# First layer's feed-forward: block products for the latents, and a second pass for the context tokens

## The chip, the cores and the metric

The kernel runs on one core of one Trainium2 chip. The metric is device microseconds of one execution. A core has five instruction streams that run beside each other and wait for each other by semaphores: PE (TensorE, matmuls), DVE (VectorE), ACT (ScalarE), POOL (GpSimd) and SP (SyncE, which here only issues DMAs). A weight load of TensorE shows as PEld.

## The reference

Two layers over 1024 noisy latent tokens and 256 context tokens of width 1024 in float32. What matters here is the feed-forward that ends each layer, and the norm at the start of the next:

```python
def modulate(x, shift, scale):
    return rms_norm(x) * (1.0 + scale) + shift

def squared_relu_mlp(h, w1, w2):                 # w1 1024 x 4096, w2 4096 x 1024
    return jnp.square(jax.nn.relu(h @ w1)) @ w2
...
    x = x + gate * squared_relu_mlp(modulate(x, shift, scale), w1, w2)
```

Shift, scale and gate come from a conditioning vector for the latents and from a second, learned one for the context (columns 0 and 1 of `mods`). The first layer's mixer is attention beside an mLSTM, the second's an RWKV-7 scan. The context is needed through the first layer's feed-forward, since the second layer's mixer reads it; after that only the latents go on.

## The kernel before

Activations lie transposed: eight tiles `xt[c]` of 128 channels by 1280 tokens (`NT`; `NL` = 1024 latents, then `NX` = 256 context tokens; `KC` = 8). Each float32 product is made of three: operands are split into a high part in fp32r (ScalarE, L94) and the remainder (GpSimd or VectorE, L95), and hi x hi, lo x hi and hi x lo are summed in PSUM. `load_w` fetches 512 KB of weights into a `raw` buffer, splits it into `wh` and `wl`, and sets `raw` free when GpSimd's subtraction is through.

Each engine runs its instructions in the order in which the program issues them; the tile pools add the waits and hand out buffers. So the order of calls in the code is the order on each engine.

- The first layer's output projection (`out0`, products `wo`) adds to x; `Stats.add` sums squares of four groups of tokens (ScalarE squares, TensorE `st` matmuls with ones), `Stats.rstd` makes a root (ScalarE), a reciprocal (VectorE), four broadcast matmuls `rb` and copies.
- The first layer's feed-forward (`mlp_layer`, `mlp`) normalizes all 1280 tokens into `h`, and walks 32 blocks of 128 hidden channels. For each block: 8 x 3 products of w1 over chunks of 512, 512 and 256 tokens (`first`, PSUM `m1`), relu and square on ScalarE, the remainder on VectorE, then 8 x 3 x 3 products of w2 (`second`, `m2`) and an update of x on VectorE (L280) for each. That makes 2 x 32 x 8 x 3 x 3 = 4608 matmuls, all at L110. The modulation weights of the next layer are woven in by a generator, `side` (`ada_w`: 32 pieces of 512 KB, products `ada`, transposes `adat`). `done` stores x to DRAM (`xd`) and sums its squares.
- `layer1_mixer` then loads constants, takes the rstd, and normalizes x in 24 pieces (`norm_h`) between the first projections of the RWKV mixer (products `po`).
- The second layer's feed-forward, on the 1024 latents alone, is `wino_mlp`: the matrices are cut into 2 x 2 blocks, and seven block products with sums and differences of blocks stand for eight (the scheme of Strassen and Winograd). `h_blocks` normalizes x and makes the seven left operands `b0..b6` (a high and a low part of four tiles each), on VectorE, ScalarE and GpSimd. `left_first` makes the right operands from w1 on GpSimd; `wino_first` (products `wa` to `we`) and `wino_second` (products `w`, blocks of w2) do 1344 matmuls of 512 columns each. The hidden blocks go through DRAM (`hd`); `wino_second` runs 64 steps, four groups `s` of 16, and adds the group's results to x at a group's end (`add`, L1260).

Of the kernel before, what the change touches and what calls it, by code (L numbers as in the profile page):

```python
# [6 lines left out]
F32 = mybir.dt.float32  # L7
# [21 lines left out]
def drain(g):  # L29
    for _ in g:  # L30
        pass
# [145 lines left out]


class Stats:

# [14 lines left out]

    def rstd(self):
# [5 lines left out]
        out = kk.slab(self.n, F32, "rstd")  # L202
        for g in range(4):
            pb = kk.bank("rb")
            kk.nc.tensor.matmul(pb[:, :q], kk.row0[32 * g:32 * g + 32, :], r4[32 * g:32 * g + 32, :], start=True, stop=True, tile_position=(32 * g, 0))
            kk.nc.scalar.activation(out[:, q * g:q * g + q], pb[:, :q], AF.Copy)
        return out
# [143 lines left out]
NB = 14  # L351
NSA = 6
# [601 lines left out]

def out0(kk, I, xt, cat, mods):
# [12 lines left out]
    return st  # L968
# [46 lines left out]
def h_blocks(kk, xt, mods, part, rstd, B):  # L1015
# [15 lines left out]
    def norm(c, i, p=None):  # L1031
        x = half(c, i)
        s1, b1 = mods[:, 8 * part + 8 + c, 0:1], mods[:, 8 * part + c, 0:1]
        V.tensor_tensor(x, x, rstd[:, 512 * i:512 * i + 512], ALU.mult)
        if p is not None:
            nc.scalar.activation(B[p][c % 4][0], x, AF.Identity, scale=s1, bias=b1)
        V.tensor_scalar(x, x, s1, b1, ALU.mult, ALU.add)
        if p is not None:
            low(p, c % 4, x)
# [136 lines left out]
def wino_second(kk, w2, hd, late, pool, xr, gate, done):  # L1176
# [64 lines left out]
    ready = [operands(0), operands(1)]  # L1241
    for c in range(KC):
        nc.sync.dma_start(xt[c], xr[c])
    g1 = lambda c: gate[:, c, 0:1]
    for i, (s, f) in enumerate(steps):
        load(i + LO2)
        if i + 2 < len(steps):
            ready.append(operands(i + 2))
# [9 lines left out]
        def add(c, h, t):  # L1258
            x = xt[c][:, 512 * h:512 * h + 512]
            V.scalar_tensor_tensor(x, t, g1(c), x, ALU.mult, ALU.add)  # L1260
            return x
        for c in range(4):
            if s == 0:
                A.activation(u[c], banks[0][c], AF.Copy)
            elif s in (1, 2):
                V.tensor_tensor(u[c], banks[0][c], u[c], ALU.add)  # L1266
        for c in range(4):
            if s == 0:
                V.tensor_tensor(v[c], banks[1][c], u[c], ALU.add)
                done(add(c, 0, v[c]), c, 0)  # L1270
            elif s == 1:
                A.activation(v[c], banks[1][c], AF.Copy)
                add(c, 1, v[c])
                add(c, 1, u[c])
            elif s == 2:
                t = kk.tmp([128, 512], "r12", bufs=2)
                V.tensor_tensor(t, u[c], banks[1][c], ALU.subtract)  # L1277
                done(add(4 + c, 0, t), 4 + c, 0)
                add(4 + c, 1, u[c])
                done(add(4 + c, 1, v[c]), 4 + c, 1)  # L1280
            else:
                done(add(c, 1, banks[0][c]), c, 1)
        banks = None


def wino_mlp(kk, X, xt, mods, w1, w2, stats, xr, done):

# [32 lines left out]

def norm_h(kk, xt, mods, h, rstd):

    nc = kk.nc
    for c in range(KC):
        for z in (0, 257, 1282):
            nc.gpsimd.memset(h[c][:, z:z + 1], 0.0)
        for a, b, cond, to in ((NL, NT, 1, 1), (0, 512, 0, 258), (512, NL, 0, 770)):
            t, o = stage(kk, b - a), h[c][:, to:to + b - a]
            nc.vector.tensor_tensor(t, xt[c][:, a:b], rstd[:, a:b], ALU.mult)
            s1, b1 = mods[:, 8 + c, cond:cond + 1], mods[:, c, cond:cond + 1]  # L1330
            if c in NP:
                nc.vector.tensor_scalar(o, t, s1, b1, ALU.mult, ALU.add)
            else:
                nc.scalar.activation(o, t, AF.Identity, scale=s1, bias=b1)
        xt[c] = None
        yield


# [783 lines left out]
def build_full(tc, I, out):  # L2122
    nc = tc.nc
    with tc.tile_pool(name="cst", bufs=1) as cst, tc.tile_pool(name="ps", bufs=8, space=PS) as ps, tc.tile_pool(name="dr", bufs=1, space=DRAM) as dr:
        kk = setup(tc, I, cst, ps, dr)
        cat = layer0_all(kk, I)
        xd = dr.tile([8, 128, NT], F32, name="xd")
        X = tc.alloc_tile_pool(name="X", reuse_waits="tile", bufs=KC)
        with tc.tile_pool(name="W2", reuse_waits="tile", bufs=4) as kk.W:
            xt = load_x(kk, I["xT"], X)  # L2130
            st = out0(kk, I, xt, cat, kk.mods[0])
            kk.WO.release()
            kk.CT.release()
            kk.c0.release()
            st1 = Stats(kk, NT, "mr", 4)

            def done(c):
                nc.sync.dma_start(xd[c], xt[c])
                for x in xt[c - 2:c - 1 if c < KC - 1 else KC] if c >= 2 else []:
                    st1.add(x)  # L2140
# [33 lines left out]

def layer1_mixer(kk, I, xt, X, mods, stats=None):

    tc, nc = kk.tc, kk.nc
    CP = tc.alloc_tile_pool(name="C1", reuse_waits="tile", bufs=1, side="right")
    kk.cst1 = CP
    rwkv_consts(kk, I)  # L2180
    dr, C = rwkv_dram(kk), kk.c
    Hp = tc.alloc_tile_pool(name="H1", reuse_waits="tile", bufs=1, side="right")
    h = [Hp.tile([128, 1283], F32, name="h%d" % c) for c in range(KC)]
    kk.L = X
    kk.wsz = 512
    with tc.tile_pool(name="W1", reuse_waits="tile", bufs=WB) as W, tc.tile_pool(name="XS", reuse_waits="tile", bufs=2 * XA) as S, tc.tile_pool(name="T1", reuse_waits="tile", bufs=2) as T:
        kk.W, kk.S, kk.T, kk.slab_w = W, S, T, NT
        norm = norm_h(kk, xt, mods, h, (stats or rms_of(kk, xt)).rstd())
        C["cmask"] = T.tile([128, 512], mybir.dt.bfloat16, name="cmask", tag="cmask", bufs=1)
# [228 lines left out]
```

## Time and profile before

| | us |
|---|---|
| median of three runs (lowest, highest) | 4336.38 (4334.75, 4348.33) |
| the profiled execution | 4338.47 |
| its span (first to last instruction on the core) | 4336.7 |
| TensorE busy in it | 3998.0 |
| VectorE, ScalarE, GpSimd busy | 2544.1, 1754.5, 1653.5 |
| mean granted TensorE clock | 0.946 of full speed |

A row of a timeline gives start, duration, engine, line, operation, output <- inputs, shapes and count of a merged run of like instructions, and in brackets the idle time ahead and what ended it. A row of groups gives busy us, mean ns of one, and the idle time ahead of them by what ended it. A row of waits names the tile that was waited for and the instruction that gave it: us in total, times, longest.

### The profile page before, as it was taken

What the parts mean: (1) busy time and instruction counts of PE and PEld (TensorE: products, weight loads), DVE (VectorE), ACT (ScalarE), POOL (GpSimd) and SP (SyncE); (2) the same over time, 40 slices, a digit from 0 to 9 for tenths busy, and PEclk for the clock granted to TensorE, in tenths of its full rate; (3) what the DMA queues carried; (4) which work ended last, traced back from release to release, by engine and by line L of the source; (5) the groups of instructions that cost most, each with busy time, mean ns of one, the idle gap of its engine ahead of it and who ended that gap; (6) DMA issues with size and microseconds to landing.
All of it is one profiled execution on the core that took longest, in us unless ns stands there. A gap on an engine that the chain in (4) does not pass through costs nothing. (4 is left out here: it accounts for less than half of the span.)

```text
span 4336.7 us, 71515 instructions
## 1 busy us (share of the span) xinstructions
PE 3998.0 (92%) x26893; PEld 3196.1 (74%) x26893; DVE 2544.1 (59%) x4559; ACT 1754.5 (40%) x4371; POOL 1653.5 (38%) x1827
## 2 busy tenths in 40 slices
PE   6999998998999999997989995999999996998999
PEld 3899875676777888884757764888777764787777
DVE  4320266517556666668684427677777635767673
ACT  4132365513111111125655533666656642332443
POOL 4112010114111111115533335455545325886776
PEclk9999998999999999998979996999989998999999
DMA  4414245511222111112233454445444441345653
GB/s 172 122 61 139 88 156 146 183 35 39 83 83 65 38 36 38 39 39 70 99 117 111 150 191 117 114 126 133 131 123 130 105 160 63 132 159 212 196 168 109
DMA packets 434406, 485.71 MB, mean 112 GB/s; under 512 B 154908, under 2 KB 310844, under 8 KB 434060
## 3 DMA queue, kind: packets, MB, share of 16 engines
q1 hardware_dynamic: 432908, 476.95, 35.4%
q8 instruction: 212, 3.47, 0.3%
q0 software_dynamic: 1152, 4.19, 0.2%
q14 instruction: 134, 1.10, 0.1%
HBM read 347.71 MB, written 129.12 MB: 110 GB/s over the span
## 5 line engine op out<-in xcount | busy, mean ns | idle before, releaser
L95 POOL TENSOR_TENSOR wl<-raw,wh 128x1024 fp32r<-128x1024 f32 (+1 forms) x172 | 354.9, 2067 | 1350.6 <-ACT wh L94 1307.5
L280 DVE SCALAR_TENSOR_TENSOR x<-m,mods,x 128x512 f32<-128x512 f32 (+1 forms) x768 | 467.5, 655 | 341.0 <-PE m L110 340.7
L94 ACT ACTIVATE wh<-raw 128x1024 fp32r<-128x1024 f32 (+1 forms) x172 | 153.8, 895 | 840.0 <-PE m L110 645.6
L110 PE MATMUL m<-h,wh 128*128 128x512 f32 (+1 forms) x1536 | 352.5, 362 | 12.4 <-POOL h L229 9.7
L110 PEld LDWEIGHTS m<-h,wh 128*128 128x128 f32 x1536 | 256.3, 189 | 88.9 <-issue 26.8
L1012 PE MATMUL w<-t,rh 128*128 128x512 f32 x896 | 289.8, 402 | 23.1 <-DVE t L95 12.2
L377 PE MATMUL pt<-wh,h 128*128 128x256 f32 x1600 | 289.3, 283 | 0.0
L95 POOL TENSOR_TENSOR rl<-raw,rh 128x512 fp32r<-128x512 f32 x160 | 232.8, 1459 | 89.7 <-ACT rh L94 85.3
L377 PEld LDWEIGHTS pt<-wh,h 128*128 128x128 f32 x1600 | 250.0, 192 | 0.0
L1821 DVE TENSOR_TENSOR prd<-P,R 80x31 f32<-80x31 f32 (+15 forms) x496 | 217.4, 438 | 25.7 <-POOL TT L1836 7.9
L377 PE MATMUL pt<-wl,h 128*128 128x256 f32 x800 | 226.4, 283 | 0.0
L1012 PEld LDWEIGHTS w<-t,rh 128*128 128x128 f32 x896 | 171.8, 192 | 70.5 <-DVE t L95 17.5
L1822 DVE TENSOR_TENSOR R<-R,prd 80x31 f32<-80x31 f32 (+15 forms) x496 | 216.2, 436 | 9.6
L94 ACT ACTIVATE rh<-raw 128x512 fp32r<-128x512 f32 x160 | 100.7, 632 | 281.7 <-PE w L1012 114.8
L1343 POOL TENSOR_TENSOR ss<-h 128x512 f32<-128x512 f32 (+1 forms) x128 | 153.8, 1211 | 122.0 <-DVE xt L1346 97.1
L110 PE MATMUL m<-hidh,wh 128*128 128x512 f32 (+1 forms) x768 | 198.3, 360 | 1.9 <-DVE x L280 1.9
L110 PE MATMUL m<-hidl,wh 128*128 128x512 f32 (+1 forms) x768 | 195.6, 358 | 0.4 <-DVE hidl L267 0.4
L1782 PE MATMUL G<-AR,BK 64*128 64x128 f32 x1280 | 175.6, 339 | 21.0 <-POOL AR L1771 10.2
L110 PE MATMUL m<-hidh,wl 128*128 128x512 f32 (+1 forms) x768 | 193.7, 357 | 0.0
L110 PE MATMUL m<-h,wl 128*128 128x512 f32 (+1 forms) x768 | 192.9, 358 | 0.0
L1789 DVE TENSOR_TENSOR G<-G,c_gmask 128x512 f32<-128x512 f32 (+1 forms) x160 | 98.8, 630 | 149.9 <-PE G L1782 149.8
L1012 PE MATMUL w<-t,rl 128*128 128x512 f32 x448 | 178.7, 399 | 0.2 <-POOL rl L95 0.2
(708 smaller groups left out, 10446.7 us busy)
## 6 DMA issues: line engine op xcount, KB each, us to landing
raw<-in_w SPq DMA_DIRECT2D x98, 512.0 KB
araw<-in_ada_w SPq DMA_DIRECT2D x80, 512.0 KB
kar<-rw_kar SPq DMA_DIRECT2D x64, 384.0 KB
css<-rw_css SPq DMA_DIRECT2D x80, 256.0 KB
hd<-t SPq DMA_DIRECT2D x64, 256.0 KB
raw<-in_w SPq DMA_DIRECT2D x64, 256.0 KB
r<-hd SPq DMA_DIRECT2D x55, 256.0 KB
hd<-r SPq DMA_DIRECT2D x48, 256.0 KB
```

What stands on the lines that cost most here:

```text
L94: self.nc.scalar.activation(hi, raw, AF.Copy)
L95: (eng or self.nc.gpsimd).tensor_tensor(lo, raw, hi.bitcast(F32), ALU.subtract)
L110: mm(o[:M, :b - a], ww, xx[:, a:b], start=(first and p == 0), stop=(last and p == 2))
L280: V.scalar_tensor_tensor(xt[c][:, u:v], p[:, u - a:v - a], gate[:, c, cond:cond + 1], xt[c][:, u:v], ALU.mult, ALU.add)
L377: mm(ps[:, :n], xx[:, sl], ww[:, k % 4, :], start=(k == 0 and p == 0), stop=(k == KC - 1 and p == 2))
L1012: kk.nc.tensor.matmul(o, ww, xx, start=(first and p == 0), stop=(last and p == 2), skip_group_check=True)
L1343: nc.gpsimd.tensor_tensor(S, h[:, q - 1:q - 1 + w], h[:, q + 1:q + 1 + w], ALU.add)
L1782: nc.tensor.matmul(pg[h][:, 128 * j:128 * j + 128], BK[HH[h], j, :], AR[HH[h], j, :], start=True, stop=True)
L1789: V.tensor_tensor(G[:, :, h, 0:m], ps.rearrange("q (c t) -> q c t", t=128)[:, :, 0:m], mask[:, :, 0:m], ALU.mult)
L1821: V.tensor_tensor(pr, P3[:, s, s + 1:32].unsqueeze(1).to_broadcast([n_, w, n]), R3[:, 0:w, s].unsqueeze(2).to_broadcast([n_, w, n]), ALU.mult)
L1822: V.tensor_tensor(R3[:, 0:w, s + 1:32], R3[:, 0:w, s + 1:32], pr, ALU.add)
```

## The change

The first layer's feed-forward is cut in two.

- `out0` holds latents and context of x in separate tiles (`Cols`), sums squares of both apart, and stores both to DRAM (`xs`) through GpSimd's queue.
- The latents go through `wino_mlp`. The rstd of the context is computed behind `h_blocks` and stored in DRAM (`rc`). Finished latents are stored to `xd`.
- `layer1_open` issues the mixer's constants, opens its pools and loads the latents of the next layer from `xd`.
- `ctx_mlp` does the 256 context tokens: w1 and w2 are loaded and split a second time, 32 blocks of 24 + 24 matmuls of 256 columns, the sums over w2 staying in four PSUM banks. The modulation generator runs in it, and `mixer.lat()`: sums of squares, rstd and norm of the next layer's latents. Then x of the context is updated, stored, summed and normalized (`mixer.ctx`).
- In the shared code, which serves both layers: 16 scale-and-shift operations of `h_blocks` go from VectorE to ScalarE. In `wino_second` the loads of x are issued at steps 4 to 11 and not ahead of the loop; most adds are put in a list, `later`, of which each following step takes two; one subtraction from PSUM becomes an addition with the negated gate.

```diff
-            mlp_layer(kk, xt, NT, kk.mods[0], I["w1_0"], I["w2_0"], SEG0, st, ada_w(kk, 1, I["ada_w"], range(NA - 8, 12)), done)
-        d = layer1_mixer(kk, I, xt, X, kk.mods[1], st1)
+        wino_mlp(kk, X, [x.lat for x in xt], kk.mods[0], I["w1_0"], I["w2_0"], st[0], xs,
+                 lambda x, c, h: nc.sync.dma_start(xd[c][:, 512 * h:512 * h + 512], x), (st[1], rc))
+        X, xt, mixer = layer1_open(kk, I, xd)
+        ctx_mlp(kk, xt, kk.mods[0], I["w1_0"], I["w2_0"], xs, rc, xd, ada_w(kk, 1, I["ada_w"], range(NA - 8, 12)), mixer)
+        d = layer1_mixer(kk, I, X, mixer)
...
# out0
-            st = Stats(kk, NT)
-            for x in behind(out_proj(kk, I["w_out"], iter(parts), xt, NT, mods, 2, SEG0, kk.ww), 1):
-                st.add(x)
+            st = Stats(kk, NL), Stats(kk, NX)
+            for c, x in enumerate(behind(out_proj(kk, I["w_out"], iter(parts), xt, NT, mods, 2, SEG0, kk.ww), 1)):
+                st[0].add(x.lat)
+                st[1].add(x.ctx)
+                kk.nc.gpsimd.dma_start(xs[c][:, :NL], x.lat)
+                kk.nc.gpsimd.dma_start(xs[c][:, NL:], x.ctx)
...
# wino_mlp
         h_blocks(kk, xt, mods, 3, stats.rstd(), B)
+        if also:
+            t = kk.S.tile([128, NX], F32, name="rc")
+            also[0].rstd(t)
+            tc.nc.sync.dma_start(also[1], t)
...
# h_blocks
-        V.tensor_scalar(x, x, s1, b1, ALU.mult, ALU.add)
+        nc.scalar.activation(x, x, AF.Identity, scale=s1, bias=b1)
...
# wino_second
-    for c in range(KC):
-        nc.sync.dma_start(xt[c], xr[c])
...
     for i, (s, f) in enumerate(steps):
         load(i + LO2)
+        if 4 <= i < 4 + KC:
+            nc.sync.dma_start(xt[i - 4], xr[i - 4][:, :NL])
+        for _ in range(2):
+            if later and i % 16 < 15:
+                later.pop(0)()
...
# ctx_mlp, wh and wl with four buffers, raw with two
+        for f in range(33):
+            load2(f + 1)
+            load1(f + 2)
+            if f < 32:
+                first(f)
+            if f >= 1:
+                last(f - 1)
+            next(side, None)
+            if f % 2:
+                next(side, None)
+            next(lat, None)
```

Where the orders change, at the places that matter here:

TensorE from the last output projection to the first product of the first layer's feed-forward; before, `m` are its products, and `rb` the broadcast of rstd over all tokens.

```order
L110 MATMUL wo<-ch,wl 128x512 x2
L110 MATMUL wo<-ch,wl 128x256
L193 MATMUL st<-sq,ones 32x320 x8
L205 MATMUL rb<-r_9275,row_78 128x320 x4
L110 MATMUL m_9431<-h,wh 128x512 x2
```

After, with the root `r_9570` of the latents and `r_9695` of the context:

```order
L110 MATMUL wo<-ch,wl 128x256
L214 MATMUL st<-sq,ones 32x256 x4
L214 MATMUL st<-sq,ones 32x64 x4
L214 MATMUL st<-sq,ones 32x256 x4
L214 MATMUL st<-sq,ones 32x64 x4
L227 MATMUL rb<-r_9570,row_78 128x256 x4
L227 MATMUL rb<-r_9695,row_78 128x64 x4
L1038 MATMUL wa<-b00h,rh 128x512
```

VectorE after, at the end of `h_blocks` (L1051 and L1080 are its remainders and differences) and the start of `wino_first` (L1141):

```order
L1051 TENSOR_TENSOR b43l<-n_9663,b43h 128x512
L1051 TENSOR_TENSOR b61l<-x_8449,b61h 128x512
L1080 TENSOR_TENSOR x_8453<-x_8453,x_8469 128x512
L1051 TENSOR_TENSOR b30l<-x_8445,b30h 128x512
L1080 TENSOR_TENSOR x_8457<-x_8457,x_8473 128x512
L1051 TENSOR_TENSOR b32l<-x_8453,b32h 128x512
L222 RECIPROCAL r_9695<-r_9695 128x64
L1141 TENSOR_TENSOR r_9801<-wb,c_9757 128x512
```

The reciprocal of the context stands behind the whole of `h_blocks` on VectorE, and the matmuls that use it stand ahead of the first product on TensorE.

SyncE at the end of the first layer's feed-forward; before, the constants and then the mixer's weights follow the stores of x:

```order
L2138 DMA xd<-x_8446 128x1280
L2138 DMA xd<-x_8448 128x1280
L2080 DMA c_mu<-in_mu 128x48
...
L2080 DMA c_gmask<-in_gmask 128x256
L90 DMA raw<-in_rkv 128x512 x6
```

After, `raw<-in_w_0` is the first weight of the context's pass:

```order
L2283 DMA xd<-x_12294 128x512
L2223 DMA c_mu<-in_mu 128x48
...
L2223 DMA c_gmask<-in_gmask 128x256
L2330 DMA x_15135<-xd 128x1024
...
L2330 DMA x_15149<-xd 128x1024
L1330 DMA rc<-rc 128x256
L1332 DMA xc<-xs_8428 128x256
...
L1332 DMA xc<-xs_8435 128x256
L90 DMA raw<-in_w_0 128x1024 x2
```

The loads of x, of the context and of its rstd stand ahead of those weights.

ScalarE in the first feed-forward; before, two splits (`wh`) to five operations on one block of the hidden channels:

```order
L94 ACTIVATE wh<-raw 128x1024 x2
L261 ACTIVATE mr<-m_13513 128x512
L261 ACTIVATE mr<-m_13514 128x512
L262 ACTIVATE hidh<-mr 128x512 x2
L261 ACTIVATE mr<-m_13515 128x256
L262 ACTIVATE hidh<-mr 128x256
L94 ACTIVATE wh<-raw 128x1024 x2
```

After, in the context's pass (`cr` relu, `chh` square, `sq` the squares of the next layer's latents):

```order
L94 ACTIVATE wh<-raw 128x1024
L1364 ACTIVATE chh<-cr 128x256
L94 ACTIVATE wh<-raw 128x1024 x2
L1363 ACTIVATE cr<-c_15465 128x256
L1364 ACTIVATE chh<-cr 128x256
L156 ACTIVATE adasb<-ada 128x512
L94 ACTIVATE wh<-raw 128x1024
L213 ACTIVATE sq<-x_15135 128x256 x2
L213 ACTIVATE sq<-x_15137 128x256
L94 ACTIVATE wh<-raw 128x1024
```

Relu and square of one block stand behind the splits of later weights, and the squares of the latents stand between them.

More of the change, by code (lines that the diff above doesn't have):

```diff
@@ L176, in ada_w, with __init__, __getitem__, load_cols @@
     return ada_steps(kk, l, w, blocks, raw, lambda: kk.W.tile([128, 512], F32, tag="adasb", name="adasb", bufs=1), sum(4 if t[0] == "w" else 2 for t in tags) - 1)
+class Cols:
+    def __init__(self, lat, ctx):
+        self.lat, self.ctx = lat, ctx
+    def __getitem__(self, ix):
+        p, c = ix
+        return self.ctx[p, c.start - NL:c.stop - NL] if c.start >= NL else self.lat[p, c]
+def load_cols(kk, src, X, XC):
+    xt = []
+    for c in range(KC):
+        x = Cols(X.tile([128, NL], F32, tag="S", name="x%d" % c), XC.tile([128, NX], F32, tag="S", name="xc%d" % c))
+        kk.nc.sync.dma_start(x.lat, src[c][:, :NL])
+        kk.nc.sync.dma_start(x.ctx, src[c][:, NL:])
+        xt.append(x)
+    return xt
 class Stats:
@@ L194, in add, with rstd @@
         self.c += 1
-    def rstd(self):
+    def rstd(self, out=None):
         kk, q = self.kk, self.q
@@ L201, in rstd @@
         kk.nc.vector.reciprocal(r4, r4)
-        out = kk.slab(self.n, F32, "rstd")
+        if out is None:
+            out = kk.slab(self.n, F32, "rstd")
         for g in range(4):
@@ L952, in layer0, with out0 @@
     return cat
-def out0(kk, I, xt, cat, mods):
+def out0(kk, I, xt, cat, mods, xs):
     with kk.tc.tile_pool(name="O", reuse_waits="tile", bufs=8) as S:
@@ L1261, in add, with fin @@
             return x
+        def fin(c, h, t, end=True):
+            x = add(c, h, t)
+            if end:
+                done(x, c, h)
         for c in range(4):
@@ L1288, in wino_mlp @@
+def wino_mlp(kk, X, xt, mods, w1, w2, stats, xr, done, also=None):
     tc = kk.tc
@@ L1318, with __init__, piece, lat @@
 CKS, CKL = chunks(NT), chunks(NL)
[L1321 to L1335, printed above, removed]
-        yield
+class Mixer:
+    def __init__(self, kk, xt, mods, h, pool):
+        self.kk, self.xt, self.mods, self.h = kk, xt, mods, h
+        self.rstd = Cols(pool.tile([128, NL], F32, name="rstl"), pool.tile([128, NX], F32, name="rstc"))
+    def piece(self, c, a, b, cond, to):
+        kk, nc = self.kk, self.kk.nc
+        t, o = stage(kk, b - a), self.h[c][:, to:to + b - a]
+        nc.vector.tensor_tensor(t, self.xt[c][:, a:b], self.rstd[:, a:b], ALU.mult)
+        s1, b1 = self.mods[:, 8 + c, cond:cond + 1], self.mods[:, c, cond:cond + 1]
+        if c in NP:
+            nc.vector.tensor_scalar(o, t, s1, b1, ALU.mult, ALU.add)
+        else:
+            nc.scalar.activation(o, t, AF.Identity, scale=s1, bias=b1)
+    def lat(self):
+        kk = self.kk
+        for _ in range(3):
+            yield
+        for c in range(KC):
+            for z in (0, 257, 1282):
+                kk.nc.gpsimd.memset(self.h[c][:, z:z + 1], 0.0)
+        st = Stats(kk, NL)
+        for c in range(KC):
+            st.add(self.xt[c][:, :NL])
+            yield
+        st.rstd(self.rstd.lat)
+        yield
+        for c in range(KC):
+            self.piece(c, 0, 512, 0, 258)
+            self.piece(c, 512, NL, 0, 770)
+            yield
+    def ctx(self, st):
+        st.rstd(self.rstd.ctx)
+        for c in range(KC):
+            self.piece(c, NL, NT, 1, 1)
 def mix_piece(kk, C, h, c, s, q, w, hi, lo, eng):
@@ L2127, in build_full @@
         xd = dr.tile([8, 128, NT], F32, name="xd")
+        xs = [dr.tile([128, NT], F32, name="xs%d" % c, tag="xs%d" % c) for c in range(KC)]
         X = tc.alloc_tile_pool(name="X", reuse_waits="tile", bufs=KC)
+        XC = tc.alloc_tile_pool(name="XC", reuse_waits="tile", bufs=KC)
         with tc.tile_pool(name="W2", reuse_waits="tile", bufs=4) as kk.W:
-            xt = load_x(kk, I["xT"], X)
-            st = out0(kk, I, xt, cat, kk.mods[0])
+            xt = load_cols(kk, I["xT"], X, XC)
+            st = out0(kk, I, xt, cat, kk.mods[0], xs)
             kk.WO.release()
@@ L2172, in rms_of, with layer1_open, layer1_mixer @@
     return st
-def layer1_mixer(kk, I, xt, X, mods, stats=None):
+def layer1_open(kk, I, xd):
     tc, nc = kk.tc, kk.nc
-    CP = tc.alloc_tile_pool(name="C1", reuse_waits="tile", bufs=1, side="right")
-    kk.cst1 = CP
+    kk.cst1 = tc.alloc_tile_pool(name="C1", reuse_waits="tile", bufs=1, side="right")
     rwkv_consts(kk, I)
-    dr, C = rwkv_dram(kk), kk.c
+    X = tc.alloc_tile_pool(name="X", reuse_waits="tile", bufs=KC)
     Hp = tc.alloc_tile_pool(name="H1", reuse_waits="tile", bufs=1, side="right")
     h = [Hp.tile([128, 1283], F32, name="h%d" % c) for c in range(KC)]
+    xt = []
+    for c in range(KC):
+        x = X.tile([128, NT], F32, tag="S", name="x%d" % c)
+        nc.sync.dma_start(x[:, :NL], xd[c][:, :NL])
+        xt.append(x)
+    m = Mixer(kk, xt, kk.mods[1], h, Hp)
+    m.pool = Hp
+    return X, xt, m
+def layer1_mixer(kk, I, X, mixer):
+    tc, nc = kk.tc, kk.nc
+    CP, Hp, h = kk.cst1, mixer.pool, mixer.h
+    dr, C = rwkv_dram(kk), kk.c
+    mixer.xt = None
     kk.L = X
@@ L2187, in layer1_mixer @@
         kk.W, kk.S, kk.T, kk.slab_w = W, S, T, NT
-        norm = norm_h(kk, xt, mods, h, (stats or rms_of(kk, xt)).rstd())
+        norm = iter(())
         C["cmask"] = T.tile([128, 512], mybir.dt.bfloat16, name="cmask", tag="cmask", bufs=1)
```

90 lines of the change are left out of this document (75 added, 15 removed).

## The prediction

> **What bounds the kernel now.** I read the page first (busy shares), then tables of windows over the feed-forward stages, then their first and last instructions, then the waits of TensorE in the second layer's feed-forward, which already runs the block products. Columns of a windows row: stretch, length, busy us and instruction count of each engine, granted clock, DMA share, GB/s.
>
> ```profile
> PE 3998.0 (92%) x26893; PEld 3196.1 (74%) x26893; DVE 2544.1 (59%) x4559; ACT 1754.5 (40%) x4371; POOL 1653.5 (38%) x1827
> 974.26 0.74 PE L110 MATMUL wo<-ch,wl 128*128 128x512 f32 x3
> 1040.00:1400.00 360.00, 358.07 (x1776) 274.06 (x1775) 210.25 (x360) 57.86 (x96) 54.83 (x23) 1.00 0.24 77
> 1400.00:1800.00 400.00, 400.00 (x2047) 339.59 (x2046) 260.48 (x432) 68.59 (x113) 67.64 (x29) 1.00 0.13 39
> L151 PE MATMUL ada<-araw,cs 128*32 128x512 f32 x128 | 33.7, 605 | 0.0
> L159 PE MATMUL adat<-ident,adasb 128*128 128x128 f32 x32 | 4.8, 271 | 0.0
> 1957.43 0.74 PE L110 MATMUL m<-hidh,wl 128*128 128x512 f32 x3
> 1976.39 0.80 PE L1390 MATMUL po<-xh,wh 128*128 128x512 f32 x1 [9.52 <-ACT xh L1347]
> 3740.00:3940.00 200.00, 200.00 (x885) 165.64 (x883) 132.02 (x128) 61.74 (x105) 162.98 (x116) 1.00 0.47 158
> ```
>
> TensorE is 92% busy, and in the stretch that the change rewrites it is the bound almost without a gap. The first layer's feed-forward runs from its last output projection (the first timeline row, which ends at 975.0) to its last product (1957.43 + 0.74 = 1958.2): **983.2 us**. Without side work it does 2047 matmuls in 400 us, 0.1954 us each (427 columns on average). The next layer's modulation, woven in between 1040 and 1400, takes 33.7 + 4.8 us, about 40 with its edges. In the other layer a 512-column matmul of the block products takes 200 / 885 = 0.226 us.
>
> **The change, step by step.** The sum is made against the profiled execution, 4338.5 us (span 4336.7), which is 2.1 us above the median of the runs shown, 4336.4. About 0.3% of that, 13 us, can be told from no change.
>
> (1) Matmul work. Removed: 4608 x 0.1954 = 900 us. Added for the 1024 latents: 2 x 1344 products of 512 columns, 2688 x 0.226 = 607; for the 256 context tokens 32 x 48 = 1536 matmuls of 256 columns. Their price is in the first layer's projections, where the same shape runs with a new weight load each time:
>
> ```profile
> 204.00:502.00 298.00, 298.00 (x2492) 297.78 (x2490) 40.17 (x76) 87.36 (x234) 47.80 (x20) 1.00 0.28 93
> L377 PE MATMUL pt<-wh,h 128*128 128x256 f32 x1600 | 289.3, 283 | 0.0
> L377 PE MATMUL pt<-wl,h 128*128 128x256 f32 x800 | 226.4, 283 | 0.0
> L377 PEld LDWEIGHTS pt<-wh,h 128*128 128x128 f32 x1600 | 250.0, 192 | 0.0
> ```
>
> 2400 of the 2492 matmuls in 298 us are these: at most 0.124 us each (the 283 ns is one matmul's own, overlapped, length). 1536 x 0.124 = 190 us. Pure TensorE work falls by 900 - 797 = 103 us; what decides is how much of it comes back as waits.
>
> Were the weight loads not hidden behind the products, each would add the 250.0 / 1600 = 0.156 us of the last row, 240 us in all; the first row speaks against it, with loads beside matmuls for 297.78 of 298 us. A rule of the Trainium skill speaks for it: TensorE: Matmul & The Clock Gate, section LDWEIGHTS (loading the stationary operand), gives columns / 1.2 ns for a load, and that page's list of what overlaps lets a load overlap running matmuls only where the row groups differ; by it the context's products would take an estimated 107 + 107 = 213 ns each, 328 us. By that rule 2400 products could not have stood in these 298 us, so the trace decides against it.
>
> (2) The start of the latents' pass. The same code stands in the other layer, so its rows price it.
>
> ```profile
> 3617.67 0.63 PE L110 MATMUL wo<-cth,wl 128*128 128x512 f32 x2
> 3626.90 6.78 DVE L1034 TENSOR_TENSOR x<-x,rstd 128x512 f32<-128x512 f32 x4 [1.48 <-ACT rstd L206]
> 3637.71 1.22 PE L1012 MATMUL wa<-b00h,rh 128*128 128x512 f32 x2 [11.51 <-ACT b00h L1036]
> 3702.06 0.80 PE L1012 MATMUL wa<-b50h,rh 128*128 128x512 f32 x1 [5.83 <-ACT c L1123]
> 3618.00:3702.00 84.00, 40.02 (x122) 24.99 (x120) 74.25 (x58) 33.09 (x57) 71.63 (x46) 0.68 0.17 56
> L1037 DVE TENSOR_SCALAR x<-x,mods 128x512 f32<-128x512 f32 x16 | 18.6, 1180 | 4.0 <-ACT b00h L1036 4.0
> 4332.54 0.39 PE L1012 MATMUL w<-t,rl 128*128 128x512 f32 x1
> 4330.88 2.85 DVE L1260 SCALAR_TENSOR_TENSOR x<-w,mods,x 128x512 f32<-128x512 f32 x4 [30.59 <-PE w L1012]
> ```
>
> From the last projection (ends at 3618.3) to the last product (4332.54 + 0.39 = 4332.9) the block products take 714.6 us; the first 96 are done at 3702.06, 83.8 us in, because VectorE is busy 74 of 84 us with h_blocks. The change takes the 16 tensor_scalars (18.6 us) from VectorE to ScalarE, which has 51 us idle there; VectorE keeps 74.25 - 18.6 - 3.2 (reciprocal and x) = 52.5 us in 39 operations. GpSimd at 71.6 of 84 then is the next in line, so of 18.6 I take 10 us in the later layer (between 3 and 15).
>
> In the first layer the same start gains a wait. The context's rstd is computed behind h_blocks, and its four broadcast matmuls stand on TensorE ahead of the first product; their operand is a reciprocal that stands behind all 39 VectorE operations. So TensorE, which now starts 19.4 us in and works beside h_blocks, would start only when VectorE is through: 8.6 us (3618.3 to 3626.9) + 3 for the context's own sums + 52.5 + 2 to 8 of waits among them (4.0 in the L1037 row) + 2 for reciprocal and broadcast = 68 to 75 us, and then do its 96 products in 21.7 + 2 (the granted clock was 0.68 in such a stretch): 92 to 99 against 83.7. I take **+12** (between 0, if it hides, and +16).
>
> (3) The second half of the block products. TensorE works 1344 x 0.226 = 304 us in 344.
>
> ```profile
> 3986.00:4020.00 34.00, 22.69 (x80) 16.96 (x79) 24.51 (x22) 9.56 (x17) 19.47 (x12) 0.80 1.02 377
> 4090.00:4110.00 20.00, 16.76 (x59) 12.44 (x58) 18.23 (x20) 5.76 (x10) 11.30 (x8) 0.83 0.56 181
> 4290.00:4332.00 42.00, 39.68 (x166) 30.45 (x165) 11.41 (x11) 12.27 (x21) 30.61 (x22) 1.00 0.13 44
> PE w L1012 <- DVE t L95: 12.2, 5, 5.9
> ```
>
> 80 matmuls need 18 of the first 34 us: 16 lost while all DMA engines are full with x, hidden blocks and weights together; 59 need 13.3 of 20: 7 lost where VectorE adds group results; 4 at the end. The change issues the x loads at steps 4 to 11 and puts off the adds, two a step. Of about 41 lost, the row of waits names 12.2 on VectorE, which the deferral can reach, and the loads perhaps half of 16; the splits of the operands stay. I take **-11** a pass (between -3 and -20), in both layers.
>
> (4) The context's pass. The weights, loaded a second time in 64 pieces of 512 KB through two raw buffers, are priced by these rows:
>
> ```profile
> 857.26 6.44 POOL L95 TENSOR_TENSOR wl<-raw,wh 128x1024 fp32r<-128x1024 f32 x2 [30.65 <-ACT wh L94]
> 863.83 1.06 ACT L94 ACTIVATE wh<-raw 128x1024 fp32r<-128x1024 f32 x1 [5.36 <-DMA raw<-in_w_out]
> 864.97 2.39 POOL L95 TENSOR_TENSOR wl<-raw,wh 128x1024 fp32r<-128x1024 f32 x1 [1.27 <-ACT wh L94]
> 867.22 1.06 ACT L94 ACTIVATE wh<-raw 128x1024 fp32r<-128x1024 f32 x1 [2.33 <-DMA raw<-in_w_out]
> 1708.18 0.38 ACT L261 ACTIVATE mr<-m 128x256 f32<-128x256 f32 x1
> 1708.60 0.42 ACT L262 ACTIVATE hidh<-mr 128x256 fp32r<-128x256 f32 x1
> 976.22 1.08 PE L193 MATMUL st<-sq,ones 128*32 128x320 f32 x4 [0.55 <-ACT sq L192]
> 977.50 1.08 PE L193 MATMUL st<-sq,ones 128*32 128x320 f32 x4 [0.20 <-ACT sq L192]
> 1966.47 0.43 SPq L2080 DMA_DIRECT2D c_gmask<-in_gmask  x1
> ```
>
> SyncE has, behind the last stores of the latents, ten constants at 0.43 us, eight x loads of 512 KB, nine context loads (1.2 MB) and only then the first weights. 5.9 MB at the 377 GB/s of the first row in (3) is 15.6 us; 0.8 for the last update (it ends at 4333.7), 3.0 for its store (the span ends that much later), 4.3 for the constants and 1.1 for a split make **25 us** without a product.
>
> TensorE needs 48 x 0.124 = 5.9 us an iteration, and 40 / 27 more, 7.4, in the 27 that carry the side. For the supply, GpSimd frees a buffer at 863.70 and its successor's split begins at 867.22: 3.5 us, then 1.06, 0.1 and 2.4: **7.1 us** round, two buffers, two pieces an iteration. So TensorE and the supply set nearly the same pace. They are tied: the w2 piece of the next iteration waits for last(f-1) to free its slot, and the relu and square of f (0.38 + 0.42) stand behind that split on ScalarE, so a late piece holds the products of the next iteration too. I take 7.7 us for 19 iterations with the side, 7.2 for the last 3, and 8.4 for 8 in which the sums of the latents add a pair of squares and matmuls that wait for each other (1.28 us from one pair to the next in the st rows, of 320 columns). The first two end 40.5 us in (25, then 8 for one paced by VectorE's norm of the context, then 7.5). 40.5 + 8 x 8.4 + 19 x 7.7 + 3 x 7.2 + 3 for the last products = **279 us** (between 260, TensorE alone with the side, and 325). First layer: 714.6 + 12 - 11 + 279 = 994.6 against 983.2: **+11**.
>
> (5) Around it. Two sets of sums in the output projection: **+2** (the sixteen stores of x go by GpSimd, which has slack there, and cost nothing unless the rstd tile waits for one of them, 2 us). From the last products to the first of the mixer: 18.2 us before, by 1958.2 and 1976.39; after, 32 short sums, a reciprocal and eight context norms, about 19: **+1**. The opening of the mixer loses its 16 norms of the latents, now beside the context's products:
>
> ```profile
> 1960.00:1990.00 30.00, 13.24 (x49) 7.40 (x47) 24.19 (x32) 16.90 (x35) 16.08 (x18) 0.66 0.28 86
> 1990.00:2040.00 50.00, 38.98 (x163) 29.24 (x163) 45.30 (x61) 28.91 (x50) 29.09 (x25) 0.90 0.08 24
> 2040.00:2090.00 50.00, 44.88 (x184) 29.47 (x184) 41.41 (x37) 35.67 (x63) 36.13 (x27) 0.93 0.23 73
> ```
>
> VectorE is full there (45 of 50 us) while TensorE lacks 16 us in the last two: **-8**, half of it (between -3 and -15). Second layer's feed-forward: -10 - 11 = **-21**.
>
> Sum: 11 + 2 + 1 - 8 - 21 = **-15**: 4323 for an execution like the profiled one, **4321** against the median.
>
> **Rivals.** *Faster: the pass of the context hides its supply.* The 2.4 us of GpSimd stretch only where VectorE works beside it, and a piece is ordered an iteration ahead; then TensorE sets the pace: 25 + 190 + 40 + 5 = 260, 19 less, 4302, and if the second halves regain 20 each, 4284. Against it: two buffers and 7.1 us a round, right at TensorE's own pace.
> *No change: the second halves regain nothing.* 377 GB/s is there with or without x, and the splits wait for hidden blocks that were just stored. Then +22: 4343.
> *Slower: two raw buffers and in-order queues set the pace of the context.* A late piece holds relu and square, these hold last(f), which holds the slot for the next piece. Each 1 us an iteration costs 31; from a mean of 8.7 against the 7.8 above it decides (4349), and at 9.1 the time is 4361. For it: the 5.36 us wait of ScalarE for a load in out0 with the same supply; against it, the next wait there is 2.33 us.
> *The weight loads don't hide*: 240 us more, 4561, by the rows of (1), which also make it 1 in 100. By the skill's rule named there it would be 138 more, 4459.
>
> **Chances.** My sum with its own range of 4305 to 4340: 0.42, a good half of it below 4323; faster rival 0.22; no change 0.17; slower 0.18; loads 0.01. That gives 0.5 faster, 0.27 within 13 us, 0.23 slower. The range 4276 to 4360 reaches to the faster and the slower rival.
>
> **What would show it.** Right: TensorE idle some 70 us between the last out projection and the first product, with a wait on the reciprocal's broadcast; 25 us idle ahead of the first context product; iterations of 7 to 8.5 us with ScalarE waiting for loads; the second layer's 96th product under 76 us after its projection. Wrong: context iterations at 6 us or above 9, or second halves that still take 344 us.

## The result, and the profile after

The changed kernel takes 4369.1 us (median of five runs, 4360.8 to 4374.0) against 4347.4 for the kernel before in the same session: a ratio of **1.0058** (95% interval 1.0037 to 1.0079), slower by 0.6%. Measured once more later it was 1.0052 (1.0031 to 1.0073). The forecast was 4321, within 4276 to 4360.

Page of the changed kernel, first part (busy time and share of each engine), and the windows of the context's pass from its first to its last product:

```profile
PE 3920.3 (90%) x26653; PEld 3137.9 (72%) x26653; DVE 2495.9 (57%) x4040; ACT 1952.6 (45%) x4753; POOL 2194.2 (50%) x2192
1733.60:1996.70 263.10, 244.34 (x1772) 204.02 (x1772) 119.61 (x120) 112.65 (x182) 160.28 (x66) 0.97 0.56 187
```

TensorE is busy 78 us less than before (3998.0), and the span is 30 us longer (4367.0 against 4336.7): the work left and waits of 108 us came. Most of them stand at the seams. Timeline of TensorE in the changed kernel, from the last output projection to the first product of the mixer:

```profile
984.68 0.74 PE L110 MATMUL wo<-ch,wl 128*128 128x512 f32 x3
...
995.52 1.24 PE L227 MATMUL rb<-r,row 32*128 32x256 f32 x8 [3.27 <-DVE r L222]
1052.65 0.80 PE L227 MATMUL rb<-r,row 32*128 32x64 f32 x8 [55.89 <-DVE r L222]
1053.38 0.80 PE L1038 MATMUL wa<-b00h,rh 128*128 128x512 f32 x1
...
1369.85 1.42 PE L1038 MATMUL w<-t,rh 128*128 128x512 f32 x3 [4.03 <-ACT rh L94]
...
1706.98 0.40 PE L1038 MATMUL w<-t,rl 128*128 128x512 f32 x1
1733.60 0.58 PE L110 MATMUL c<-hc0h,wh 128*128 128x256 f32 x1 [26.22 <-ACT wh L94]
...
2006.29 0.57 PE L214 MATMUL st<-sq,ones 128*32 128x64 f32 x4 [0.20 <-ACT sq L213]
...
2020.39 1.22 PE L1533 MATMUL po<-xh,wh 128*128 128x512 f32 x2 [11.07 <-ACT wh L94]
```

The reader sees three seams: 55.9 us until the context's reciprocal, 26.2 us until the first split of the second load of the weights, and 24 us from the last context product (1996.7) to the mixer, the last 11 behind a weight that ScalarE splits after everything else.

A ledger of the two profiled executions, from first and last products as in these rows (us; the marks are starts of matmuls, so they differ by less than one from those of the prediction):

| stretch | before | after | change | forecast |
|---|---|---|---|---|
| up to the last product of the output projection | 974.7 | 985.1 | +10.4 | +2 |
| first feed-forward: first half of the blocks, against the same code in the second layer before | 372.9 | 384.8 | +11.9 | +12 |
| its second half, likewise | 342.1 | 337.5 | -4.6 | -11 |
| the whole first feed-forward, with the context's pass | 983.5 | 1011.6 | +28.1 | +11 |
| context's pass in it, with the gap ahead of it | | 289.3 | | 279 |
| last feed-forward product to first mixer product | 18.2 | 23.7 | +5.5 | +1 |
| mixer to the last product of the second output projection | 1641.5 | 1636.2 | -5.3 | -8 |
| second feed-forward, first half | 372.9 | 370.0 | -2.9 | -10 |
| its second half | 342.1 | 336.3 | -5.8 | -11 |

The changes add to +30.0, the difference of the spans. The medians differ by 21.8: the profiled execution of the kernel before was 9 us below the median of its session. Single executions also differ by several us where the code is the same. Three kernels of the next section have the old mixer and took 1633.2 to 1634.1 us in it, not 1641.5; ten have the new one and took 1620 to 1640, so the -5.3 of that row shows no gain. Four have the context's pass as it stands here and took 292.5 to 295.0 us for it with its gap, not 289.3.

### The profile page after: what moved, and what is told of

Read it like the earlier page. It is cut to its first block, busy times and chain, and to the rows that moved or that the text cites. A ratio compares the mean times of both kernels' runs of the same rounds, so it can differ in the third digit from the quotient of the medians.

```text
span 4367.0 us, 72691 instructions
## 1 busy us (share of the span) xinstructions
PE 3920.3 (90%) x26653; PEld 3137.9 (72%) x26653; DVE 2495.9 (57%) x4040; ACT 1952.6 (45%) x4753; POOL 2194.2 (50%) x2192
## 5 line engine op out<-in xcount | busy, mean ns | idle before, releaser
L1038 PE MATMUL w<-t,rh 128*128 128x512 f32 x1792 | 582.2, 402 | 35.3 <-DVE t L95 19.5
L95 POOL TENSOR_TENSOR rl<-raw,rh 128x512 fp32r<-128x512 f32 x320 | 492.6, 1550 | 118.7 <-ACT rh L94 112.4
L1038 PEld LDWEIGHTS w<-t,rh 128*128 128x128 f32 x1792 | 342.5, 191 | 135.4 <-DVE t L95 38.0
L1038 PE MATMUL w<-t,rl 128*128 128x512 f32 x896 | 356.2, 398 | 0.4 <-POOL rl L95 0.3
L400 PE MATMUL pt<-wh,h 128*128 128x256 f32 x1600 | 289.3, 283 | 0.0
L1964 DVE TENSOR_TENSOR prd<-P,R 80x31 f32<-80x31 f32 (+15 forms) x496 | 218.6, 441 | 25.4 <-DMA P<-ga 10.5
L1038 PEld LDWEIGHTS w<-t,rl 128*128 128x128 f32 x896 | 171.6, 192 | 38.3 <-POOL rl L95 1.9
L1925 PEld LDWEIGHTS G<-AR,BK 64*128 64x128 f32 x1280 | 123.1, 215 | 53.3 <-issue 16.7
L2021 PE MATMUL px<-UV,G 128*64 128x64 f32 x1280 | 143.9, 237 | 12.4 <-DVE G L1932 8.9
L400 PEld LDWEIGHTS pt<-wl,h 128*128 128x128 f32 x800 | 153.6, 192 | 0.0
L1489 DVE SCALAR_TENSOR_TENSOR xt<-ss,c_hmu,xt 128x512 f32<-128x512 f32 (+1 forms) x128 | 123.5, 981 | 30.3 <-ACT xt L1488 22.4
L1142 DVE SCALAR_TENSOR_TENSOR r<-r 128x512 f32<-128x512 f32 x128 | 134.7, 1053 | 4.2
```

The costliest lines, as they stand in the source:

```text
L95: (eng or self.nc.gpsimd).tensor_tensor(lo, raw, hi.bitcast(F32), ALU.subtract)
L400: mm(ps[:, :n], xx[:, sl], ww[:, k % 4, :], start=(k == 0 and p == 0), stop=(k == KC - 1 and p == 2))
L1038: kk.nc.tensor.matmul(o, ww, xx, start=(first and p == 0), stop=(last and p == 2), skip_group_check=True)
L1142: V.scalar_tensor_tensor(t, t, 0.0, t, ALU.max, ALU.mult)
L1489: nc.vector.scalar_tensor_tensor(t, S, C["hmu"][:, s, c:c + 1], t, ALU.mult, ALU.add)
L1925: nc.tensor.matmul(pg[h][:, 128 * j:128 * j + 128], BK[HH[h], j, :], AR[HH[h], j, :], start=True, stop=True)
```

## Experiments

Each experiment's profile gives its stretches; its time is compared with the kernel before on the same chip.

**The wait for the context's reciprocal.** In `wino_mlp`:

```diff
-        h_blocks(kk, xt, mods, 3, stats.rstd(), B)
+        rs = stats.rstd()
         if also:
             t = kk.S.tile([128, NX], F32, name="rc")
             also[0].rstd(t)
             tc.nc.sync.dma_start(also[1], t)
+        h_blocks(kk, xt, mods, 3, rs, B)
```

> The changed kernel with the context's rstd computed ahead of h_blocks instead of behind it. Theory (the reciprocal that stands behind h_blocks on VectorE holds TensorE's first product): the 55.9 us wait of the rb broadcast goes, the first product comes some 20 us after the last output projection instead of 68, and the first half of the block products in the first layer takes about 369 us from the last projection, as in the second layer of the changed kernel (369.6), against 384.5: about 15 us less in all, 4354. Rival (left and right operands are ready no earlier, so the wait moves to them one for one): first half unchanged at 384, time unchanged at 4369.

Measured: 1.0021 (1.0005 to 1.0036), median 4345.7. TensorE in it, timeline and then waits of the first half in the first layer:

```profile
996.36 1.24 PE L227 MATMUL rb<-r,row 32*128 32x256 f32 x8 [3.27 <-DVE r L222]
1011.01 0.80 PE L227 MATMUL rb<-r,row 32*128 32x64 f32 x8 [13.41 <-DVE r L222]
1011.74 0.80 PE L1038 MATMUL wa<-b00h,rh 128*128 128x512 f32 x1
```

```profile
PE we L1038 <- ACT rh L94: 18.5, 1, 18.5
PE rb L227 <- DVE r L222: 16.7, 2, 13.4
```

The first product comes 25.7 us after the last projection, not 68.3, but 18.5 of the 42.6 us come back as a wait for `rh`, a split of a right operand; the first half falls by 13.3 us, from 384.8 to 371.5. The theory holds in its size, but of 42.6 us only 13.3 are left. Besides the wait for `rh` and 3 us of other waits, the products themselves took longer. Windows from the first product to the first of the second half (columns as in the prediction, PE first, the granted clock behind the five engines), in this kernel and then in the changed one:

```profile
1011.74:1357.53 345.79, 315.54 (x1347) 256.82 (x1345) 259.50 (x234) 118.80 (x203) 284.49 (x184) 0.95 0.42 143
1053.38:1369.85 316.47, 307.95 (x1346) 252.63 (x1344) 212.25 (x200) 91.74 (x160) 245.47 (x163) 1.00 0.46 156
```

TensorE is busy 7.6 us longer for the same 1344 products, at a mean granted clock of 0.95 against 1.00.

**The edit of h_blocks alone**, in the kernel before (second layer only):

```diff
-        V.tensor_scalar(x, x, s1, b1, ALU.mult, ALU.add)
+        nc.scalar.activation(x, x, AF.Identity, scale=s1, bias=b1)
```

> The kernel before with one part of the change alone: the 16 scale-and-shift operations of h_blocks on ScalarE, in the second layer's feed-forward. My prediction had 10 us less (first half 368.6 to 358). Theory now (ScalarE's splits of the right operands, rh, are ordered behind the operations added to it, and TensorE waits for them): first half within 2 us of 368.6, with one wait of TensorE for rh of some 20 us, as in the changed kernel; time unchanged at about 4347. Rival (that wait belongs to another part of the change): first half 356 to 361 and no long wait for rh.

Measured: first half 369.6 us (-3.3), time 0.9982 (0.9971 to 0.9993). Waits of TensorE in that half, first in this kernel and then in the changed kernel (second layer); the kernel before has no wait for `rh` there:

```profile
PE wd L1012 <- ACT rh L94: 20.1, 1, 20.1
PE wa L1012 <- ACT b00h L1036: 11.4, 1, 11.4
```

```profile
PE wd L1038 <- ACT rh L94: 20.2, 1, 20.2
PE wa L1038 <- ACT b00h L1062: 11.4, 1, 11.4
```

ScalarE in the changed kernel shows what `rh` stood behind:

```profile
3720.36 0.63 ACT L1054 ACTIVATE b32h<-x 128x512 fp32r<-128x512 f32 x1 [3.43 <-DVE x L1080]
3720.90 0.61 ACT L94 ACTIVATE rh<-raw 128x512 fp32r<-128x512 f32 x1
3721.56 0.63 ACT L1054 ACTIVATE b33h<-x 128x512 fp32r<-128x512 f32 x1
```

The order of ScalarE's instructions says the same. Between `b00h` and `b33h` stood ten splits of right operands before and one after: the section on the kernel was too simple when it said that the order of calls is the order on each engine. Splits that are called after `h_blocks` stand ahead of its operations and between them, and with sixteen more operations on ScalarE hardly any stood between. The edit alone still made the kernel some 0.2% faster, where I had expected no change.

The wait for `rh` is not the whole account, though. The same product, the 193rd, in the kernel before and in the changed kernel (the last projections start at 3617.90 and 3656.64):

```profile
3725.57 0.39 PE L1012 MATMUL wa<-b50h,rh 128*128 128x512 f32 x1
3755.44 0.39 PE L1038 MATMUL wa<-b50h,rh 128*128 128x512 f32 x1
```

It comes 107.7 us after the projection before and 98.8 after, so the start gained 8.9 us in spite of that wait. From there to the second half TensorE takes 265.2 us before and 271.2 after: 6 of the 8.9 us are lost again. The runs agree on both: in the four kernels without the edit in this layer it is 107.6 to 108.9 and then 265.2 to 265.6, in the nine with all sixteen operations on ScalarE 97.6 to 99.0 and then 269.9 to 274.1. Just behind the start, in the changed kernel, ScalarE waits for a difference of weight blocks that GpSimd makes, and the copy of a result that TensorE waits for stands behind it:

```profile
3761.93 0.63 ACT L94 ACTIVATE rh<-raw 128x512 fp32r<-128x512 f32 x1 [5.82 <-POOL raw L1105]
3763.09 0.50 PE L1038 MATMUL wa<-b60h,rh 128*128 128x512 f32 x1 [2.05 <-ACT u L1149]
```

Such waits of TensorE for `u` add to 2.5 us in that stretch, where it had none before. What takes the rest of the 6 us is not traced.

**The edit of the second half alone**, in the kernel before (x loads at steps 4 to 11, adds put off):

> The kernel before with the other shared part alone: x loads at steps 4 to 11 and adds put off, in the second half of the second layer's block products. Theory: the second half falls from 346 us to about 336, as in the changed kernel, with the same waits for t and rh, and the time by 10 us (0.2%). Rival (the second half gained in the changed kernel because h_blocks or the place in memory changed too): no change, 346.

Measured: second half 340.5 us against 342.1; 0.9989 (0.9979 to 0.9999). What TensorE waits for there before, and then with the edit:

```profile
PE w L1012 <- DVE t L95: 12.2, 5, 5.9
PE w L1012 <- DVE v L1269: 3.2, 3, 2.1
```

```profile
PE w L1013 <- DVE t L95: 12.1, 6, 5.9
PE w L1013 <- DVE v L1280: 1.3, 2, 0.8
```

The deferral took 2 us off the wait for `v`, whose group's adds it moves. The wait for `t`, which I gave to the adds and the loads, is unchanged. The 10 us that I expected did not come. In the changed kernel and its nine variants the same code takes 336.0 to 338.4 us in this layer, and 336.0 is the variant without the edit of `h_blocks`; where the other 2 to 4 us come from is open. VectorE in that kernel, ahead of the `t` that TensorE waits 5.9 us for:

```profile
3990.94 0.69 DVE L1222 TENSOR_TENSOR raw<-raw,k 128x512 f32<-128x512 f32 x1 [0.22 <-DMA k<-in_w]
...
3995.25 1.81 DVE L1218 TENSOR_TENSOR q<-q,k 128x512 f32<-128x512 f32 x1 [1.33 <-POOL rl L95]
3996.98 1.78 DVE L1222 TENSOR_TENSOR raw<-raw,k 128x512 f32<-128x512 f32 x1
3998.69 1.79 DVE L1218 TENSOR_TENSOR q<-q,k 128x512 f32<-128x512 f32 x1
4000.40 3.46 DVE L1224 TENSOR_TENSOR q<-q,raw 128x512 f32<-128x512 f32 x2
...
4008.81 1.75 DVE L95 TENSOR_TENSOR t<-r,t 128x512 fp32r<-128x512 f32 x1
```

It is busy without a gap with sums of weight blocks from 3995 to 4010, each 1.75 us instead of 0.69. The Trainium skill (SBUF — State Buffer, section SBUF: two separate sides) says that a VectorE instruction with two inputs in SBUF and a GpSimd instruction that reads SBUF contend for a pair of ports, held by one of them for its whole instruction. GpSimd makes remainders all through that stretch, and none beside the instruction of 0.69 us; 0.69 against 1.75 us agrees.

To test it, the kernel before with the low part of the second hidden block on GpSimd for the first four steps:

```diff
-            kk.split(x, hi, lo, V if j else P)
+            kk.split(x, hi, lo, V if j and i > 3 else P)
```

> The kernel before with one thing changed: in the first four steps of the second half, the low part of the second hidden block is taken on GpSimd instead of VectorE, where it stands behind sums and differences of weight blocks (L1217 to L1223, 1.75 us each). Theory (these sums on VectorE, not the loads of x or the adds to x, make TensorE's wait of 5.9 us for t at the start of the second half): that wait falls below 3 us and the second half from 342 to 337 us. Rival (the hidden block itself comes late from DRAM, behind the loads of x): a wait of 5 to 6 us remains there, for t of GpSimd, and 342 us.

Measured: the wait of 5.9 us is gone and waits of 2.5, 0.5 and 0.4 us for GpSimd's `t` stand in the same steps; the second half takes 340.8 us against 342.1, not 337. So VectorE's sums did make that wait, and the x loads did not. The product that had waited 5.9 us starts 16.0 us after the first of the half instead of 18.8, and the 73rd 24.8 instead of 28.4, but 2 of these 3.6 us are lost again later in the half. The time, 0.9984 (0.9972 to 0.9996), fell by more than this stretch shows.

**The sixteen operations back on VectorE**, in the changed kernel, the reverse of the h_blocks edit in both layers:

> The changed kernel with the 16 operations of h_blocks back on VectorE, in both layers. Theory: in the first layer TensorE starts only when VectorE is through with h_blocks, so its first product comes about 15 us later (68 to 83 us after the last projection) and the first half takes 390 to 400 us against 384.5; in the second layer the first half stays at 369; 4375 to 4385 in all. Rival (the splits of the right operands bind in the first layer too): first half in the first layer unchanged at 384 or lower, time unchanged.

Measured: 1.0098 (1.0083 to 1.0114), 4383.0. First product 76.2 us after the last projection, first half 394.2 us, and in the second layer 372.7:

```profile
1062.11 0.80 PE L227 MATMUL rb<-r,row 32*128 32x64 f32 x8 [63.87 <-DVE r L222]
```

So in the changed kernel most of the edit's worth lies in the first layer (9.4 us against 2.7), where it shortens a wait that the same change had brought.

**The short sums.** `Stats` with one group of 256 context tokens instead of four of 64, in the output projection and behind the context's pass:

```diff
-            st = Stats(kk, NL), Stats(kk, NX)
+            st = Stats(kk, NL), Stats(kk, NX, groups=1)
...
-        sc = Stats(kk, NX)
+        sc = Stats(kk, NX, groups=1)
```

> The changed kernel with the context's sums of squares as one group of 256 tokens (one square and one matmul a channel tile) instead of four of 64. Theory (the short sums cost time: in out0, whose last projection ends 10 us later than before, and behind the context's last products, where 16 merged pairs take 12 us from 1995 to 2007.6): from the last context product to the first product of the mixer 15 to 18 us instead of 24, and the last output projection 3 to 5 us earlier; 8 to 12 us less in all. Rival (the weights of the mixer, which TensorE waits for there, bind anyway; the projection is late for other reasons): tail unchanged at 24, time unchanged.

Measured: last context product to mixer 18.1 us instead of 23.7, the output projection's end at 981.0 instead of 985.1; 1.0032 (1.0015 to 1.0049). The sums themselves fell from 12 us to these:

```profile
1997.77 4.42 PE L214 MATMUL st<-sq,ones 128*32 128x256 f32 x16
2004.53 0.69 PE L227 MATMUL rb<-r,row 32*128 32x256 f32 x2 [2.33 <-DVE r L222]
2016.12 1.22 PE L1533 MATMUL po<-xh,wh 128*128 128x512 f32 x2 [10.90 <-ACT wh L94]
```

In the six kernels of this study with the short sums the last product of the output projection starts at 985 to 991 (mean 987.4), in the four with one group at 978 to 983 (980.6), and in the four with the old projection at 975 to 979 (977.1): the +10.4 of the ledger belongs to the change, and one group takes two thirds of it away.

**The order on SyncE's queue.** The next layer's x and the mixer's constants behind the context's loads and its first weights:

```diff
# layer1_open
-    rwkv_consts(kk, I)
...
-        nc.sync.dma_start(x[:, :NL], xd[c][:, :NL])
# ctx_mlp
         load2(0)
         load1(1)
+        for c in range(KC):
+            nc.sync.dma_start(xt[c][:, :NL], xd[c][:, :NL])
+        rwkv_consts(kk, mixer.I)
```

> The changed kernel with the mixer's constants and the loads of the next layer's x issued behind the context's loads and its first two weights, not ahead of them. Theory (the order on SyncE's queue and 4.7 MB ahead of the first weights make the 26.2 us wait at the start of the context's pass): that wait falls to 10 to 14 us and the time by 12 us. Rival (it is the chain of the context's own norm: its loads, VectorE, ScalarE): the wait stays above 22 us, or falls while the first iterations get longer by as much.

Measured: 1.0022 (1.0006 to 1.0039). The wait falls to 13.5 us:

```profile
PE c L110 <- ACT wh L94: 15.3, 2, 13.5
PE c L1380 <- DVE chl L1369: 12.3, 8, 2.5
```

From the last block product to the last context product it is 286 us against 289.3, though: the first four iterations take 44.2 us instead of 37.9, since the loads now stand in the middle of the first weights. The second half of the rival was half right: 6.3 of the 12.7 us came back there. Against the other four kernels with the unchanged pass (292.5 to 295.0 us) the new order is worth 7 to 9 us.

**More raw buffers** in the context's pass, four instead of two:

> The changed kernel with four raw buffers for the weights of the context's pass instead of two. My prediction's rival had the two buffers as the pace from 8.7 us an iteration. Theory now (TensorE is the pace: 244 of the 263 us from the first to the last context product are busy, with the modulation and the latents' sums in them): the 263 us fall by less than 8, time within 8 us of 4369. Rival (a late piece holds ScalarE and with it the hidden block): 263 falls to 245, 18 us less.

```profile
1743.10:1994.80 251.70, 241.22 (x1772) 202.91 (x1772) 124.53 (x120) 112.99 (x182) 164.36 (x66) 0.97 0.58 195
```

Measured: 251.7 us instead of 263.1, 1.0011 (0.9993 to 1.0028). That is between theory and rival. Of the 11.4 us, 8.3 are idle time of TensorE and 3.1 busy time; 10.5 us of idle time stay. In the other four kernels with the unchanged pass this stretch took 265.9 to 268.6 us, so the two more buffers are worth 11 to 17 us. The larger part of the pace is TensorE's own work, 241 to 244 us.

**The mends together**, with seven splits of right operands called ahead of h_blocks:

> All three mends together: the context's rstd ahead of h_blocks, one group for the context's sums, the context's loads first; and seven splits of the right operands put ahead of h_blocks in both layers, which ScalarE did six of ahead of it. If the parts add, 13 to 16 + 8 to 12 + 12 us less than the changed kernel, and 0 to 10 more by the seventh split: 4325 to 4336, that is 5 to 15 us below the kernel before (4341). If they hide each other, 4341 to 4350.

Measured: 0.9983 (0.9962 to 1.0003), 4344.3: not clear of no change, and short of the sum of the parts. The seventh split brought nothing (first halves 374.6 and 368.7 us; 16.5 us of waiting for `rh` stay in the first).

**The changed kernel again**, beside the last two:

> The changed kernel once more, unchanged, beside the two that follow, since its runs spread: between 1.003 and 1.007 of the kernel before, if the first measurement (1.0058) holds.

Measured: 1.0052 (1.0031 to 1.0073), 4367.9.

**The mends, four raw buffers, and the loads spread** (x one tile an iteration, constants at iteration 20):

```diff
         for f in range(33):
             load2(f + 1)
             load1(f + 2)
+            if f < KC:
+                nc.sync.dma_start(xt[f][:, :NL], xd[f][:, :NL])
+            if f == 20:
+                rwkv_consts(kk, mixer.I)
```

> The mends of e7_all, with four raw buffers in the context's pass, and the loads of the next layer's x spread over its first eight iterations, the constants at iteration 20. Theory (e6 lost its gain because those loads stood in the middle of the first weights; e9 gained 11 us of waits for weights): first context product 13 us after the last block product, as in e6_ctx_early, the first four iterations 35 to 38 us instead of 46, and 245 to 250 us in all from the first to the last context product; 10 to 20 us less than e7_all, 4325 to 4335 with the kernel before at 4345. Rival (the latents' sums wait for their x instead): iterations 3 to 10 get longer, no gain on e7_all.

Measured: **0.9953** (0.9939 to 0.9968), 4324.4 us against 4342.1: faster than both kernels. The stretch from the last projection to the mixer takes 999.9 us (1035.3 in the changed kernel, 1001.7 before):

```profile
1707.90 0.58 PE L111 MATMUL c<-hc0h,wh 128*128 128x256 f32 x1 [13.57 <-ACT wh L95]
1707.90:1962.00 254.10, 241.41 (x1770) 203.87 (x1771) 129.16 (x125) 113.16 (x182) 164.23 (x66) 0.97 0.60 207
```

The first four iterations take 41.2 us and the pass 254, 4 us above what was expected.

**Half of h_blocks' operations on each engine**, on top of that:

```diff
-        nc.scalar.activation(x, x, AF.Identity, scale=s1, bias=b1)
+        if c % 2:
+            V.tensor_scalar(x, x, s1, b1, ALU.mult, ALU.add)
+        else:
+            nc.scalar.activation(x, x, AF.Identity, scale=s1, bias=b1)
```

> The same as e10_best with the 16 operations of h_blocks shared: odd channel tiles on VectorE, even ones on ScalarE, so that splits of the right operands are ordered among them. Theory (the first half is held by the splits that stand behind h_blocks on ScalarE): the wait of TensorE for rh of 18 to 20 us falls below 8, and the first halves take 360 to 366 us in place of 374.6 and 368.7: 10 to 18 us less than e10_best. Rival (VectorE and the left operands set the pace then): first halves within 3 us of 372.

Measured: 0.9955 (0.9941 to 0.9968), first halves 375.8 and 370.4 us, as in the kernel just above (375.7 and 373.2). The rival held, but for 0.8 us in the first layer. There the wait for `rh` fell to 3.1 us and waits for left operands took its place; in the second it stayed:

```profile
PE we L1039 <- ACT rh L95: 14.2, 1, 14.2
```

What would shorten the first half further is left open: neither half of the operations back on VectorE nor one more early split does.

## Why the prediction was wrong

The matmul prices held. In the changed kernel 164 matmuls, 156 of them the context's products, take 20.00 us, 0.122 us each where 0.124 was taken:

```profile
1960.00:1980.00 20.00, 20.00 (x164) 19.03 (x163) 6.82 (x8) 8.25 (x12) 13.22 (x6) 1.00 0.42 132
```

- *Step 2, first layer:* right in its mechanism; that the size fits so well is in part luck. The first product came after 68.3 us (68 to 75 forecast), and the first experiment gave back 13.3 us. But the start cost 7 us at the 97th product (91.1 us against 83.8, where 8 to 15 were forecast). The half is 11.9 us longer because the products from the 193rd on take 271.5 us against 265.2, which the sum did not have.
- *Step 2, second layer, -10:* failed in taking the gain of the start for the gain of the half. The product that I timed at 83.8 us (it is the 97th, behind a wait of 5.8 us; the 96th had ended before that) came at 76.6 us, where I wanted under 76, and the 193rd came 8.9 us earlier. But the 1152 products behind the start took 6 us longer than before: -2.9 in the profile, -3.3 with the edit alone. I had named GpSimd as the next in line and priced nothing for it behind the start, and it stands behind the first of the new waits. I had also named ScalarE's 51 us of idle time as the cover and not asked what stood in it: ten splits, nine of which went behind the operations that it took over and made a wait of 20 us.
- *Step 3, -11 a pass:* failed in size; -4.6 and -5.8 in the changed kernel, -1.6 with the edit alone. I read the first 34 us of that half by its DMA share and the waits for `t` by the name of the engine. What VectorE did in that time, sums of weight blocks, its timeline would have told; relieving it of one operand there was worth 1.3 us of the half. (The half took 342.1 us before, not the 344 of the prediction.)
- *Step 4:* 289.3 for 279, and 292.5 to 295.0 in four other kernels with the same pass. The gap was right (26.2 for 25). Per iteration it was 8.15 us where I had 7.84, and both things I tied together count: 241 to 244 us are TensorE's, of which the products make some 190, and two raw buffers instead of four cost 11 to 17 us. The slower rival, a pass held by its supply above 8.7 us an iteration, did not happen.
- *Step 5:* the output projection ended 10 us later, not 2, and the end of the context's pass cost 5.5 us more, not 1. I gave no working for the short sums. They are squares and matmuls that wait for each other, 0.64 to 0.77 us for two of each; one group instead of four took two thirds of the first cost and all of the second away, and the last third is not traced. The mixer's gain of 8 us is not shown at all.

No rival happened as such; that of second halves which regain nothing was half right (-10.4 of the -22 in both). Between the -15 us of the sum and the +30 of the two profiled executions lie 45 us. Gains of the block products that did not come make 19 of them (-32 forecast, -13.3 measured), the small costs at the seams 13 (+3 for +16), the context's pass 10 and the mixer 3. All missed in one direction, and the range was built from the context's pass.

## What to carry to other kernels

Splitting a pass to save matmul work adds seams, and each seam costs what its first operand needs: price every seam from the queue order on each engine, and look at the order on the engine that *receives* the moved work, since its idle time may be the place of somebody else's operands. A gain at the start of a stretch is the gain of the stretch only if nothing behind it is waiting to become the limit. A wait named after an engine is explained only by that engine's own timeline. And a small helper on a fifth of the tokens cost half or more of what it costs on all of them here.

## What the runs showed of the hardware

ScalarE squares and TensorE sums that wait for each other get cheaper far less than their width: two of each follow the two before every 0.64 to 0.77 us with 64 columns, against 1.28 us with 320 in the kernel before. Loads that merely stand in the same queue moved the first wait of the context's pass by 12.7 us (26.2 to 13.5), and half of that came back, 6.3 us more in the first four iterations.
